# Moving weight loads, bias rows and the output weights' squares along the schedule of a two-layer attention and retention trunk

## Chip, cores and metric

The kernel runs on one core of one Trainium2 chip. The metric is the device time of one execution, in microseconds (us); lower is better. A profile of one execution stands beside the timed runs. Engines: PE is TensorE (matmuls), PEld its weight loads, ACT ScalarE, DVE VectorE, POOL GpSimd, SP SyncE, which here issues nearly all DMAs and so is called the DMA queue.

## What is computed

A sequence of 2048 tokens of width 1024 passes through two layers, and each layer is

```
h = rms_norm(x, norm_gain)                         # over the 1024 columns
aq, ak, av, ag, rq, rk, rv, rg = split(h @ w_in)   # eight sections of 512 columns
A = softmax(aq ak^T / 8 + bias, band) av           # 8 heads of 64, chunks of 64, own chunk + 8 before
B = rms_norm(retention(rotary(rq), rotary(rk), rv))# 4 heads of 128, decaying state, per head
x = x + concat(A * silu(ag), B * silu(rg)) @ w_out
```

and a last RMS norm follows. The bias of a head depends on the distance between two tokens, clipped at 256, and is looked up in a small table. Sums are wanted at float32 accuracy.

## The kernel before

**Numbers in two halves.** Matmuls run in float16. Every float32 operand is scaled by a power of two and split into an upper half and a rest (whT and wlT, hTh and hTl), and three products replace one: upper by upper, upper by rest, rest by upper. So each weight section needs, before its use, a load of 512 KB into a staging ring of three buffers (w4, L46), a square with its sum (sumsq, L308: ACT writes the squares at L312), a sum over partitions on PE and a scale (allsum, L322), and a conversion: upper half on ACT (L333), rest on DVE (L336).

**Stages.** The projection is cut into four slices s of the sections (each two attention heads and one retention head) and four strips n of 512 tokens. For each layer l, slice s and strip n there are two stages: dense_T(l,s,n) (L624; queries and keys, transposed; matmuls at L748) and dense_V(l,s,n) (L755; values and gates; L767). Each has four groups of 24 matmuls 128x512, yields after a third of a group, and so has 12 rounds. After the last slice comes the output projection wout (L1071, matmuls at L1110), which reads the finished rows y (tiles yyy, of 128 tokens), squares, scales, splits and transposes them, and multiplies with the output weights whO and wlO.

**Rounds.** run (L1157) goes through the rounds of a stage. In each it runs what is due of the deferred pieces (later, L607; tick, L610), one step of the attention and retention of the stage before (attention, L793; retention, L879), and then pulls steps from generators that were handed over with push (L1133), evenly over the number of rounds given as run's last argument. The engines PE, ACT, DVE and POOL execute in the order in which the program was written by these rounds; each is in order. SP is ordered by a scheduler, which may draw a DMA ahead to where its buffer is free, unless the DMA was marked to stay in program order (in_turn, L593). SP itself is also in order: a DMA that waits for its source or its buffer holds up all behind it, and each also waits until its lane, one of eight, is free.

**One attention unit** (three rounds) makes 128x640 scores S on PE into a single PSUM buffer (L815, L816), adds the bias on DVE (L819), takes the exponential on ACT (L822), copies to float16 (L824, ACT), takes the rest (L825, POOL), transposes both halves by DMA into pT (L827, SP), and multiplies with the values two units later (L835 to L837). The bias tile of a head is built by a DMA that lays the table out in DRAM (toep, L567), a DMA that reads it with a skewed pattern, two memsets and a scaling on ACT (bias_tiles, L574). **One retention tile** (six rounds) makes a product on PE, masks it (L888), splits it into dT (ACT L873, DVE L877) and uses it a few rounds on as an operand at L869; the state's halves sh go through the same lines.

**Who is pushed where** (main loop, L1377 and on). At n = 1, prep_T (L385) of the next slice, or prep_O(0) (L521) after the last: the four weight sections of dense_T, or the first half of the output weights. At n = 3, prep_V (L417) of the next slice, or prep_O(1). At s = 2, n = 2, prep_Omax (L497): it reads the first 1024 columns of w_out in eight loads of 512 KB, squares each, adds the sums on DVE (L507, L509), and makes the scale of the output weights. At s = 3, n = 3, wout_first (L1058): it loads the first two rows tiles of y, squares, scales and splits them and transposes the first (y_turn, L971). tables (L83) makes the rotary sines and cosines in slice 0.

Of the kernel before, what the change touches and what calls it, by code (L numbers as in the profile page):

```python
# [27 lines left out]
def hybrid_trunk(ctx: ExitStack, tc: tile.TileContext, x, pos, gain, gcol, w_in, w_out, rel, fgain,  # L28
# [54 lines left out]
    def tables(n, wk):  # L83

        ang, k, r, k2 = wk
        pi = k2.bitcast(I32)
        for hf in range(2):
            o = n * 512 + hf * 256
            sp.dma_start(pi[hf * 64:(hf + 1) * 64, :], pos[None, o:o + 256].to_broadcast([64, 256]))
        yield  # L90

        def mulsub(dst, kk, c):
            dve.scalar_tensor_tensor(out=dst, in0=kk, scalar=-c, in1=dst, op0=ALU.mult, op1=ALU.add)

        def rnd(dst, src, mul):
            dve.tensor_scalar(dst, src, mul, MAGIC, op0=ALU.mult, op1=ALU.add)
            dve.tensor_scalar(dst, dst, -MAGIC, None, op0=ALU.add)

        act.activation(ang, pi, AF.Copy, scale=invf_sb[:, 0:1])
        yield  # L100
        rnd(k, ang, 1.0 / P1)
        yield
        for c in (PA, PB, PC):
            mulsub(ang, k, c)
            yield
        dve.scalar_tensor_tensor(out=k2, in0=k, scalar=-(PD + PE_), in1=ang, op0=ALU.mult, op1=ALU.add)
        yield
        rnd(k2, k2, 1.0 / TWO_PI)
        yield
        for kk, c in ((k2, QA), (k, PD), (k2, QB), (k, PE_), (k2, QC)):  # L110
            mulsub(ang, kk, c)
            yield
        dve.tensor_scalar(ang, ang, PI_CL, -PI_CL, op0=ALU.min, op1=ALU.max)
        yield
        dve.scalar_tensor_tensor(out=k, in0=ang, scalar=-1.0, in1=ang, op0=ALU.mult, op1=ALU.max)
        yield
        act.activation(r, ang, AF.Sin)
        act.activation(k2, k, AF.Sin, scale=-1.0, bias=quarter[:, 0:1])
        yield
        act.activation(ang, r, AF.Copy, scale=-1.0)  # L120
        yield
        for hf in range(2):
            sl = slice(hf * 64, hf * 64 + 64)
            cs = slice(hf * 256, hf * 256 + 256)
            sp.dma_start(tab_d[n][0, 0:64, cs], k2[sl, :])
            sp.dma_start(tab_d[n][0, 64:128, cs], k2[sl, :])
            sp.dma_start(tab_d[n][1, 0:64, cs], ang[sl, :])
            sp.dma_start(tab_d[n][1, 64:128, cs], r[sl, :])
        tab_done.add(n)
        yield  # L130
# [158 lines left out]
    TSEC = (0, 1, 4, 5)  # L289
    VSEC = (2, 6, 3, 7)  # L290

    def load_sec(src, nm, halves=False):

        v = src.rearrange("(k p) c -> p k c", p=P)
        if not halves:
            st = w4.tile([P, KT, P], F32, tag="w4", name=f"st{nm}")
            sp.dma_start(st, v)
            return [(st, 0, KT)]
        h = KT // 2
        st = [b2.tile([P, 3 - i, 512], F16, tag=("rot2", "rot3")[i], name=f"st{nm}_{i}") for i in range(2)]  # L300
        st = [t_[:, 0:2].rearrange("p a c -> p (a c)").bitcast(F32).rearrange("p (k c) -> p k c", c=P) for t_ in st]
        for i in range(2):
            sp.dma_start(st[i], v[:, i * h:(i + 1) * h, :])
        return [(st[i], i * h, (i + 1) * h) for i in range(2)]
# [49 lines left out]
    class Sections:  # L354
# [11 lines left out]

        def load(self, j):
            o = TSEC[j] * 512 + self.s * P
            self.sts.append(load_sec(w_in[self.l, :, o:o + P], f"{self.nm}{j}", self.halves))

        def square(self, j):
            nm = f"{self.nm}{j}"
# [12 lines left out]
    def prep_T(l, s, g, halves=False, w=None):  # L385
        w = w or Sections(l, s, g, halves)
        w.load(0)
        yield
        for j in range(4):
            if j < 3:  # L390
                w.load(j + 1)
            yield
            w.square(j)
            yield
            yield
            yield
            w.scale(j)
            yield from w.split(j)
# [122 lines left out]
    def prep_O(l, c, g, go):  # L521
        nm = f"O{l}_{c}"
        g.vh = b3.tile([P, KT, 512], F16, tag="wh", name=f"wh{nm}")
        g.vl = b3.tile([P, KT, 512], F16, tag="wl", name=f"wl{nm}")
        sts = [load_sec(w_out[l, :, c * 512:c * 512 + P], f"{nm}0")]
        yield
        for j in range(4):
            if j < 3:
                o = c * 512 + (j + 1) * P
                sts.append(load_sec(w_out[l, :, o:o + P], f"{nm}{j + 1}"))  # L530
            yield from convert(sts[j], g.vh[:, :, j * P:(j + 1) * P], g.vl[:, :, j * P:(j + 1) * P], go.os)
# [75 lines left out]
    def later(k, fn):  # L607
        deferred.append([k, fn])
# [449 lines left out]
    def wout_first(l, go, us):  # L1058
        us.append(y_load(l, 0))
        x_load(l, us[0])  # L1060
        us.append(y_load(l, 1))
        u, v = us
        for fns in ((), (lambda: y_squares(l, u),), (lambda: y_scale(u, go),), (lambda: rows_hi(u.rows, u.y, u.sy),),
                    (lambda: rows_lo(u.rows, u.y, u.sy), lambda: y_squares(l, v)), (lambda: y_turn(u), lambda: y_scale(v, go)),
                    (lambda: rows_hi(v.rows, v.y, v.sy),), (lambda: rows_lo(v.rows, v.y, v.sy),)):
            yield
            for fn in fns:
                fn()
        yield

    def wout(l, go, gc, us, wT=None):  # L1071

# [303 lines left out]
    for l in range(DEPTH):  # L1376
        gO = [Grp(), Grp()]  # L1377
        go = Grp()
        for s in range(NSW):
            g = grp(l, s)  # L1380
            for n in range(NS):
                first = (l, s, n) == (0, 0, 0)
                if not first:
                    st = St()
                    states[l, s, n] = st
                    dT = dense_T(l, s, n, g, st)
                else:
                    st = st0
                if n == 0 and not first:
                    bs, bt = bias_scratch(l, s), bias_tiles(l, s, g)  # L1390
                    later(1, lambda bs=bs: next(bs))
                    for k in (6, 10, 17, 21):
                        later(k, lambda bt=bt: next(bt))
                if (l, s) == (0, 0) and 0 < n < NS - 1:
                    if n == 1:
                        push(t1, TAB_STEPS - 7)
                    pairs = [xs0[0], w4.tile([P, D], F32, tag="w4", name="rows8") if n == 1 else xs0[1]]
                    pairs = [(w_[:, 0:D], w_[:, D:2 * D]) for w_ in (r_.bitcast(F16) for r_ in pairs)]
                    push(norms_from_input(range(4 * n + 4, 4 * n + 8), late[0:4] if n == 1 else None, pairs,
                                          tables(n + 1, [xs0[n + 1][:, i * 256:(i + 1) * 256] for i in range(4)])), 21)  # L1400
                if (l, s, n) == (0, 1, 1):
                    for l_ in range(1, DEPTH):
                        gr = gain_scale(l_)
                        later(2, lambda gr=gr: next(gr))
                        later(10, lambda gr=gr: next(gr))
                        later(18, lambda gr=gr: next(gr))
                if n == (NS - 1 if (l, s) == (0, 0) else 1):
                    if s + 1 < NSW:
                        push(prep_T(l, s + 1, grp(l, s + 1)), 25)
                    else:  # L1410
                        push(prep_O(l, 0, gO[0], go), 9)
                if n == NS - 1 and s == 1 and l + 1 < DEPTH:
                    gain_load(l + 1)
                if not first:
                    run(dT, att, 10 if n == 0 else 14 if (l, s, n) == (0, 0, NS - 1) else 22 if (l, s) == (0, 0) else 24)
                if n == NS - 1 and s == NSW - 1:
                    us = []
                    push(wout_first(l, go, us), 10)
                if n == 2 and s == 2:
                    push(prep_Omax(l, go), 13)  # L1420
                if n == NS - 1:
                    if s + 1 < NSW:
                        push(prep_V(l, s + 1, grp(l, s + 1)), 23)
                    else:
                        push(prep_O(l, 1, gO[1], go), 9)
                run(dense_V(l, s, n, g, st), att, 24 if n == NS - 1 and s < NSW - 1 else 12)
                if first:
                    sp_order.__exit__(None, None, None)
                    ring["free"] = True
                if att[0] is not None:  # L1430
                    drain(att[0])
                att = [attention(l, s, n, g, st, states.get((l, s, n - 1)))]
# [84 lines left out]
```

## Time and profile before

| | us |
|---|---|
| median of 3 runs | 2080.15 |
| lowest and highest | 2079.01, 2080.17 |
| profiled execution, own time | 2082.83 |
| its span | 2081.1 |
| PE busy | 2006.5 (96% of the span) |
| DVE, ACT, POOL busy | 1229.8, 1139.5, 683.5 |
| mean granted TensorE clock | 0.991 |
| PE waits for pT from DMA | 12.3, in 11 waits |

Times inside the profile count from the span's start. The stages that matter here start at: dense_V(0,1,0) 280.5, dense_T(0,2,2) 563.4, dense_V(0,2,2) 589.3, dense_T(0,3,3) 823.0, dense_V(0,3,3) 849.0, the output projection of layer 0 877.9, dense_T(1,1,0) 1268.8, dense_T(1,2,0) 1474.8, dense_V(1,2,2) 1604.8. A group's row gives line, engine, operation, written and read tiles, and the number and length of its instructions; in a timeline the last bracket is the time for which the engine had been idle and what it waited for. SPq in a timeline is the issue of a DMA on SP, not its transfer; "DMA to landing" is the time from issue to the end of the transfer.

### The profile page before, as it was taken

The numbers are of one execution on the slowest core, as the hardware profiler recorded it, in microseconds if no ns is written. First come the engines' busy times: TensorE is split into PE (matmuls) and PEld (weight loads), VectorE is DVE, ScalarE is ACT, GpSimd is POOL, SyncE is SP. The second block draws the span as 40 slices with busy tenths as digits, with TensorE's granted clock in tenths as the row PEclk, the third lists the DMA queues.
The fourth block names the chain that finished last, engine by engine and source line by source line (L and its number), as shares of the span: only waits on it lengthen the run. The fifth ranks groups of instructions, "written<-read, shape, count | busy, mean of one in ns | idle before, by whom it ended". The sixth has DMA issues, their size and how long they took to land.

```text
span 2081.1 us, 39317 instructions
## 1 busy us (share of the span) xinstructions
PE 2006.5 (96%) x14014; PEld 1052.0 (51%) x14014; DVE 1229.8 (59%) x3817; ACT 1139.5 (55%) x2530; POOL 683.5 (33%) x701
## 2 busy tenths in 40 slices
PE   6988999999999999998999999999999999999998
PEld 4444545555555555544444555555555555554543
DVE  7776556566556555576653556555655565557643
ACT  7566665556565644555443546554655565446432
POOL 0244343444334434430002333444334334343100
PEclk9999999999999999999999999999999999999999
DMA  8678674547484854799765546554755776548874
GB/s 237 162 153 180 142 148 112 114 110 164 117 182 113 167 137 102 153 234 260 203 163 118 125 104 148 120 126 103 152 111 128 178 146 161 127 102 192 211 199 125
DMA packets 645701, 313.63 MB, mean 151 GB/s; under 512 B 459232, under 2 KB 602080, under 8 KB 645504
## 3 DMA queue, kind: packets, MB, share of 16 engines
q1 hardware_dynamic: 645504, 311.12, 65.5%
q8 instruction: 109, 1.79, 0.4%
q14 instruction: 88, 0.72, 0.1%
HBM read 123.26 MB, written 41.98 MB: 79 GB/s over the span
## 4 chain that ended last, share of the span: by engine, by line
PE 49%; DMA 2%; ACT 2%; DVE 1%; issue 0%; SPq 0%; POOL 0%; POOLq 0%; ACTq 0%; DVEq 0%
PE dT L748 15%; PE dV L767 14%; PE dO L1110 13%; PE r L869 2%; DMA pT<-pq 1%; PE S L816 1%; PE S L815 1%; PE o L835 1%; PE o L836 1%; PE o L837 1%; ACT stO1m L312 0%; ACT sc L822 0%; PE ptn L1011 0%; DVE sc L819 0%; ACT pq L824 0%
## 5 line engine op out<-in xcount | busy, mean ns | idle before, releaser
L825 POOL TENSOR_TENSOR pq<-sc,pq 128x640 f16<-128x640 f32 (+4 forms) x256 | 319.6, 1248 | 872.1 <-ACT pq L824 460.2
L822 ACT ACTIVATE sc<-sc,mq,cT 128x640 f32<-128x640 f32 (+4 forms) x256 | 218.4, 853 | 629.4 <-DVE rl L841 338.3
L767 PE MATMUL dV<-whV,hTh 128*128 128x512 f16 x1024 | 353.1, 381 | 4.3 <-DVE gt L785 4.2
L767 PE MATMUL dV<-wlV,hTh 128*128 128x512 f16 x1024 | 353.2, 381 | 0.0
L767 PE MATMUL dV<-whV,hTl 128*128 128x512 f16 x1024 | 353.1, 380 | 0.0
L748 PE MATMUL dT<-hTh,whT 128*128 128x512 f16 x1008 | 349.2, 382 | 2.1 <-DMA hTh<-xa 1.1
L748 PE MATMUL dT<-hTh,wlT 128*128 128x512 f16 x1008 | 348.0, 380 | 0.0
L748 PE MATMUL dT<-hTl,whT 128*128 128x512 f16 x1008 | 347.8, 380 | 0.0
L767 PEld LDWEIGHTS <-hTh 128*128 128x128 f16 x2048 | 196.8, 98 | 219.2 <-DVE gt L785 6.5
L748 PEld LDWEIGHTS <-whT 128*128 128x128 f16 x2016 | 193.0, 98 | 214.9 <-issue 10.6
L819 DVE CUSTOM_DVE_ANT_0 sc<-S,bias 128x640 f32<-128x640 f32 (+4 forms) x256 | 188.3, 736 | 112.7 <-PE S L816 111.3
L1110 PE MATMUL dO<-whO,yly 128*128 128x512 f16 x512 | 194.6, 380 | 1.5 <-DMA yly<-hTl 0.8
L1110 PE MATMUL dO<-whO,yhy 128*128 128x512 f16 x512 | 194.8, 381 | 1.0 <-DMA yhy<-hTh 1.0
L1110 PE MATMUL dO<-wlO,yhy 128*128 128x512 f16 x512 | 194.8, 380 | 0.0
L824 ACT ACTIVATE pq<-sc 128x640 f16<-128x640 f32 (+4 forms) x256 | 171.5, 670 | 8.1
L1110 PEld LDWEIGHTS <-yhy 128*128 128x128 f16 x1024 | 99.9, 98 | 116.1 <-DMA yhy<-hTh 1.5
L767 PEld LDWEIGHTS <-hTl 128*128 128x128 f16 x1024 | 99.3, 98 | 110.6 <-issue 1.9
L748 PEld LDWEIGHTS <-wlT 128*128 128x128 f16 x1008 | 97.5, 98 | 113.1 <-issue 6.2
L815 PE MATMUL S<-k,q 128*128 128x128 f16 (+3 forms) x592 | 142.9, 268 | 0.2
L835 PE MATMUL o<-v,pT 128*128 128x65 f16 x1120 | 130.0, 194 | 12.3 <-DMA pT<-pq 12.3
L836 PE MATMUL o<-v,pT 128*128 128x64 f16 x1120 | 130.2, 195 | 0.0
L816 PE MATMUL S<-k,q 128*128 128x128 f16 (+3 forms) x592 | 130.2, 268 | 0.0
(352 smaller groups left out, 3462.1 us busy)
## 6 DMA issues: line engine op xcount, KB each, us to landing
q<-qq SPq DMA_DIRECT2D x128, 128.0 KB, 2.4
yyy<-y_d SPq DMA_DIRECT2D x32, 512.0 KB, 4.7
stT<-in_w_in_dram SPq DMA_DIRECT2D x27, 512.0 KB, 5.1
stV<-in_w_in_dram SPq DMA_DIRECT2D x26, 512.0 KB, 4.7
k<-kk SPq DMA_DIRECT2D x128, 64.0 KB, 2.0
swp<-rot SPq DMA_DIRECT2D x64, 128.0 KB, 2.7
tabc<-tab SPq DMA_DIRECT2D x32, 256.0 KB, 3.0
tabs<-tab SPq DMA_DIRECT2D x32, 256.0 KB, 3.2
```

What stands on the lines that cost most here:

```text
L748: pe.matmul(ps, w_[:, j, kt, :], h_[:, kt, :], start=(m == 0), stop=(m == 23))
L767: pe.matmul(ps, h_[:, kt, a * P:(a + 1) * P], w_[:, kt, :], start=(m == 0), stop=(m == 23))
L815: pe.matmul(o, st.q[:, hx, 0, cs], k_, start=True, stop=False)
L816: pe.matmul(o, st.q[:, hx, 1, cs], k_, start=False, stop=True)
L819: dve.tensor_tensor_reduce(out=v, in0=S[:, 0:w], in1=g.bias[hx][:, 640 - w:640], scale=1.0, scalar=-3.0e38, op0=ALU.add, op1=ALU.max, accu ...
L822: act.activation(v, v, AF.Exp, bias=m[:, 0:1], scale=g.c[:, 0:1])
L824: act.activation(pq[:, 0:w], v, AF.Copy)
L825: pool.tensor_tensor(pq[:, w:2 * w], v, pq[:, 0:w], op=ALU.subtract)
L835: pe.matmul(o[:, 0:65], u.p[:, b, :], v_[:, 0:65], start=(b == 0), stop=False)
L836: pe.matmul(o[:, 0:64], u.p[:, b, :], v_[:, 65:129], start=False, stop=False)
L869: pe.matmul(out_, w_, m_, start=(i == 0), stop=(i + 1 == len(pairs)))
L1110: pe.matmul(ps, h_[:, kt, :], w_[:, kt, :], start=(m == 0), stop=(m == 23))
```

## The change

Five things move; no instruction is added or taken away on PE, ACT, DVE, POOL or SP.

- **Bias.** With n = 0, the layout of the bias table in DRAM is written two rounds later (3 instead of 1), and the two bias tiles are loaded and scaled one round later in two of four steps (7 and 11 instead of 6 and 10).
- **Held loads.** The first weight load of prep_T and of prep_O(0) is marked to stay in program order, so that the scheduler doesn't draw it ahead into the stage with n = 0; one and two more yields keep the later steps about where they were.
- **Squares of the output weights.** prep_Omax is pushed ahead of dense_T(l,2,2) instead of ahead of dense_V(l,2,2). Its 13 steps then come one a round. The queue's order follows: three of its loads stay where they were, the fourth to eighth go between the transposes, copies and table loads of dense_T, the eighth behind the transpose of the score unit of the fourth.
- **First finished rows.** wout_first is pushed ahead of dense_T(l,3,3) instead of ahead of dense_V; the transpose of the first rows tile is taken out of it and put beside prep_O(1) at round 7 of dense_V(l,3,3).
- **Tables of n = 3.** One yield less in tables: the clamp and the absolute value come in one round, and all behind it a round sooner.

```diff
@@ -111,7 +111,8 @@
             mulsub(ang, kk, c)
             yield
         dve.tensor_scalar(ang, ang, PI_CL, -PI_CL, op0=ALU.min, op1=ALU.max)
-        yield
+        if n < 3:
+            yield
         dve.scalar_tensor_tensor(out=k, in0=ang, scalar=-1.0, in1=ang, op0=ALU.mult, op1=ALU.max)
         yield
         act.activation(r, ang, AF.Sin)
@@ -289,12 +290,14 @@
     TSEC = (0, 1, 4, 5)
     VSEC = (2, 6, 3, 7)
 
-    def load_sec(src, nm, halves=False):
+    def load_sec(src, nm, halves=False, held=False):
 
         v = src.rearrange("(k p) c -> p k c", p=P)
         if not halves:
             st = w4.tile([P, KT, P], F32, tag="w4", name=f"st{nm}")
-            sp.dma_start(st, v)
+            i = sp.dma_start(st, v)
+            if held:
+                in_turn(i)
             return [(st, 0, KT)]
         h = KT // 2
         st = [b2.tile([P, 3 - i, 512], F16, tag=("rot2", "rot3")[i], name=f"st{nm}_{i}") for i in range(2)]
@@ -366,7 +369,8 @@
 
         def load(self, j):
             o = TSEC[j] * 512 + self.s * P
-            self.sts.append(load_sec(w_in[self.l, :, o:o + P], f"{self.nm}{j}", self.halves))
+            self.sts.append(load_sec(w_in[self.l, :, o:o + P], f"{self.nm}{j}", self.halves,
+                                     j == 0 and not self.halves and (self.l, self.s) > (0, 1)))
 
         def square(self, j):
             nm = f"{self.nm}{j}"
@@ -390,6 +394,8 @@
             if j < 3:
                 w.load(j + 1)
             yield
+            if j == 0 and not halves and (l, s) > (0, 1):
+                yield
             w.square(j)
             yield
             yield
@@ -522,8 +528,11 @@
         nm = f"O{l}_{c}"
         g.vh = b3.tile([P, KT, 512], F16, tag="wh", name=f"wh{nm}")
         g.vl = b3.tile([P, KT, 512], F16, tag="wl", name=f"wl{nm}")
-        sts = [load_sec(w_out[l, :, c * 512:c * 512 + P], f"{nm}0")]
-        yield
+        sts = [load_sec(w_out[l, :, c * 512:c * 512 + P], f"{nm}0", held=c == 0)]
+        yield
+        if c == 0:
+            yield
+            yield
         for j in range(4):
             if j < 3:
                 o = c * 512 + (j + 1) * P
@@ -1061,12 +1070,20 @@
         us.append(y_load(l, 1))
         u, v = us
         for fns in ((), (lambda: y_squares(l, u),), (lambda: y_scale(u, go),), (lambda: rows_hi(u.rows, u.y, u.sy),),
-                    (lambda: rows_lo(u.rows, u.y, u.sy), lambda: y_squares(l, v)), (lambda: y_turn(u), lambda: y_scale(v, go)),
+                    (lambda: rows_lo(u.rows, u.y, u.sy), lambda: y_squares(l, v)), (lambda: y_scale(v, go),),
                     (lambda: rows_hi(v.rows, v.y, v.sy),), (lambda: rows_lo(v.rows, v.y, v.sy),)):
             yield
             for fn in fns:
                 fn()
         yield
+
+    def with_turn(gen, us):
+
+        for r in range(12):
+            if r == 7:
+                y_turn(us[0])
+            next(gen, None)
+            yield
 
     def wout(l, go, gc, us, wT=None):
 
@@ -1388,8 +1405,8 @@
                     st = st0
                 if n == 0 and not first:
                     bs, bt = bias_scratch(l, s), bias_tiles(l, s, g)
-                    later(1, lambda bs=bs: next(bs))
-                    for k in (6, 10, 17, 21):
+                    later(3, lambda bs=bs: next(bs))
+                    for k in (7, 11, 17, 21):
                         later(k, lambda bt=bt: next(bt))
                 if (l, s) == (0, 0) and 0 < n < NS - 1:
                     if n == 1:
@@ -1406,23 +1423,24 @@
                         later(18, lambda gr=gr: next(gr))
                 if n == (NS - 1 if (l, s) == (0, 0) else 1):
                     if s + 1 < NSW:
-                        push(prep_T(l, s + 1, grp(l, s + 1)), 25)
+                        push(prep_T(l, s + 1, grp(l, s + 1)), 26 if s else 25)
                     else:
-                        push(prep_O(l, 0, gO[0], go), 9)
+                        push(prep_O(l, 0, gO[0], go), 11)
                 if n == NS - 1 and s == 1 and l + 1 < DEPTH:
                     gain_load(l + 1)
-                if not first:
-                    run(dT, att, 10 if n == 0 else 14 if (l, s, n) == (0, 0, NS - 1) else 22 if (l, s) == (0, 0) else 24)
-                if n == NS - 1 and s == NSW - 1:
-                    us = []
-                    push(wout_first(l, go, us), 10)
                 if n == 2 and s == 2:
                     push(prep_Omax(l, go), 13)
+                last = n == NS - 1 and s == NSW - 1
+                if last:
+                    us = []
+                    push(wout_first(l, go, us), 9)
+                if not first:
+                    run(dT, att, 12 if last else 10 if n == 0 else 14 if (l, s, n) == (0, 0, NS - 1) else 22 if (l, s) == (0, 0) else 24)
                 if n == NS - 1:
                     if s + 1 < NSW:
                         push(prep_V(l, s + 1, grp(l, s + 1)), 23)
                     else:
-                        push(prep_O(l, 1, gO[1], go), 9)
+                        push(with_turn(prep_O(l, 1, gO[1], go), us), 12)
                 run(dense_V(l, s, n, g, st), att, 24 if n == NS - 1 and s < NSW - 1 else 12)
                 if first:
                     sp_order.__exit__(None, None, None)
```

## The prediction

> **What bounds the kernel now.** The page first, its busy times:
>
> ```profile
> PE 2006.5 (96%) x14014; PEld 1052.0 (51%) x14014; DVE 1229.8 (59%) x3817; ACT 1139.5 (55%) x2530; POOL 683.5 (33%) x701
> ```
>
> TensorE is busy for 2006.5 us of a span of 2081.1. The change adds no matmul and takes none away, so what can change is the 74.6 us between matmuls and the pace of the matmuls themselves. Next, therefore, the waits of PE: who waits for what, us in total, times, longest.
>
> ```profile
> PE o L835 <- DMA pT<-pq: 12.3, 11, 2.1
> PE r L869 <- DVE dT L877: 8.1, 9, 2.1
> PE r L869 <- DVE sh L877: 8.1, 5, 4.2
> ...
> PE r L869 <- ACT dT L873: 4.3, 3, 1.5
> PE dV L767 <- DVE gt L785: 4.2, 2, 3.3
> ```
>
> What the change can win is in these: attention probabilities (pT) that come late out of their DMA transpose, and small evacuations on DVE and ACT that are late because something stands ahead of them on their engine. The stretches show where:
>
> ```profile
> 563.40:589.30 25.90, 25.90 (x197) 13.84 (x195) 15.24 (x50) 14.20 (x32) 7.21 (x7) 1.00 0.63 131
> 589.30:618.20 28.90, 26.50 (x208) 14.24 (x206) 15.57 (x51) 20.06 (x47) 13.45 (x13) 1.00 0.85 200
> 823.00:849.00 26.00, 26.00 (x203) 13.95 (x200) 13.59 (x41) 11.25 (x25) 6.57 (x7) 1.00 0.69 132
> 849.00:877.90 28.90, 26.61 (x208) 14.43 (x206) 18.73 (x56) 18.89 (x40) 15.36 (x13) 1.00 0.61 139
> 1604.80:1633.90 29.10, 26.70 (x209) 14.53 (x207) 15.06 (x51) 19.93 (x47) 13.57 (x13) 0.99 0.77 191
> 877.90:930.00 52.10, 48.40 (x358) 25.57 (x356) 36.30 (x103) 28.10 (x52) 14.42 (x12) 0.97 1.04 232
> ```
>
> After the window stand its length, busy PE, PEld, DVE, ACT and POOL, the granted clock, the DMA share and GB/s. Rows 1 and 3, dense_T(0,2,2) and dense_T(0,3,3), are full: PE never rests. The dense_V behind each of them (rows 2 and 4) loses 2.4 and 2.3 us. The change moves work from rows 2 and 4 into rows 1 and 3. By its sum ACT has room there (14.2 and 11.3 of 26); whether it has room by its order decides.
>
> **A. Bias and held weight loads: a gain.** dense_T(1,2,0), SP, then PE; after them the same wait in dense_V(0,1,0), and PE's waits between 1260 and 1310:
>
> ```profile
> 1479.76 1.16 SPq L567 DMA_DIRECT2D toep<-rel_d  x2
> 1481.02 0.53 SPq L297 DMA_DIRECT2D stT<-in_w_in_dram  x1
> 1482.27 4.46 SPq L827 DMA_TRANSPOSE pT<-pq  x1
> ```
> ```profile
> 1491.72 0.20 PE L835 MATMUL o<-v,pT 128*128 128x65 f16 x1 [1.88 <-DMA pT<-pq]
> ...
> 1493.16 0.63 PE L748 MATMUL dT<-hTh,whT 128*128 128x512 f16 x1
> ...
> 1496.56 0.38 PE L748 MATMUL dT<-hTl,whT 128*128 128x512 f16 x1
> 1496.77 0.38 PE L748 MATMUL dT<-hTh,whT 128*128 128x512 f16 x1
> ```
> ```profile
> 290.78 0.20 PE L835 MATMUL o<-v,pT 128*128 128x65 f16 x1 [2.03 <-DMA pT<-pq]
> ```
> ```profile
> PE o L835 <- DMA pT<-pq: 1.4, 1, 1.4
> ```
>
> Two bias copies and a weight load stand on SP ahead of the transpose; its issue takes 4.46 us, and PE stops for 1.88. The eight matmuls from 1493.16 to 1496.56 then take 3.40 us, where eight of 0.21 (1496.56 to 1496.77) take 1.7: another 1.7 lost. dense_V(0,1,0) loses 2.03 and, I assume, the same 1.7; dense_T(1,1,0) loses 1.4. Together 1.88 + 1.7 + 2.03 + 1.7 + 1.4 = 8.7 us. The change puts the copies behind this transpose and the weight load at the end of dense_V. The bias loads and their scaling follow a round later; their first reader is the first score unit of the next attention, more than twenty rounds on, so that costs nothing unless SP falls a whole stage behind. What is late next is a transpose that now has two weight loads right ahead of it, the last of the attention beside n = 0:
>
> ```profile
> 516.17 4.59 SPq L827 DMA_TRANSPOSE pT<-pq  x2
> ```
> ```profile
> 522.79 0.19 PE L835 MATMUL o<-v,pT 128*128 128x65 f16 x1
> ```
>
> PE reads that pT at 522.79. Issued at about 516.2 plus 1.0 for the loads (0.53 each), with the 4.46 of the first fence and landing at once, it is there at 521.7 and costs nothing; at a median landing of a weight load, 5 us behind its issue, it comes at up to 524, 1.2 late. In six places that is 0 to 7; I take 0.5 each, 3.0, nearer to the transposes' own row. A gives **−5.7** (−8.7 to −1.7).
>
> The Trainium skill, "TensorE: Matmul & The Clock Gate", section "What's actually happening", has the clock fall to half after an idle window of about 3.4 us and return after as long a busy one. The 3.40 us of slow matmuls agree with its second half; the stop of 1.88 us ahead of them is shorter than its first half asks for.
>
> **B. The output weights' squares a stage sooner: a loss.** Eight loads of 512 KB, eight squares on ACT and eight adds on DVE go from dense_V(l,2,2) to dense_T(l,2,2). Removed is what the old place loses: 28.90 − 26.50 = 2.4 us in layer 0; in layer 1 the same (29.10 − 26.70), and about 1.7 for a slow stretch behind (clock 0.99): **−6.5**. What is added is order. The squares as they run now, and the engines in the stage that gets them (ACT, DVE, POOL, SP, PE):
>
> ```profile
> L312 ACT ACTIVATE stO0m<-stO0m x8: 1039/1042/1058, 595.0 to 614.2; 128x1024 f32<-128x1024 f32 x8
> L312 ACT ACTIVATION_READ_ACCUMULATOR stO0m<-stO0m x8: 185/187/190, 596.0 to 615.1; 128x1 f32 x8
> ...
> DMA to landing us min/median/max: 4.1/4.8/7.3
> ```
> ```profile
> 572.55 0.18 ACT L930 ACTIVATION_READ_ACCUMULATOR r<-r 128x1 f32 x1
> 572.64 0.57 ACT L647 ACTIVATE qq<-dT 128x512 f16<-128x512 f32 x1
> 573.12 0.26 ACT L873 ACTIVATE dT<-r 128x128 f16<-128x128 f32 x1
> 575.99 0.92 ACT L822 ACTIVATE sc<-sc,mq,cT 128x640 f32<-128x640 f32 x1 [2.61 <-DVE rl L841]
> 576.94 0.74 ACT L824 ACTIVATE pq<-sc 128x640 f16<-128x640 f32 x1
> 577.58 0.29 ACT L917 ACTIVATE state<-state 128x128 f32<-128x128 f32 x1
> 577.78 0.58 ACT L664 ACTIVATE kk<-dT 128x512 f16<-128x512 f32 x1
> ```
> ```profile
> 574.62 0.28 DVE L877 SCALAR_TENSOR_TENSOR dT<-dT,r 128x128 f16<-128x128 f16 x1
> 574.82 0.82 DVE L819 CUSTOM_DVE_ANT_0 sc<-S,bias 128x640 f32<-128x640 f32 x1
> ```
> ```profile
> 577.80 1.40 POOL L825 TENSOR_TENSOR pq<-sc,pq 128x640 f16<-128x640 f32 x1 [3.49 <-ACT pq L824]
> ```
> ```profile
> 573.38 1.32 SPq L827 DMA_TRANSPOSE pT<-pq  x1
> ```
> ```profile
> 588.80 0.28 PE L869 MATMUL r<-rv,dT 128*128 128x128 f16 x2
> ```
>
> A square is 1.04 + 0.19 = 1.23 us. Its staging ring has three buffers, ACT, DVE and SP run in order, and in the changed order the pieces hang on each other. The first square follows the read at 572.73 and ends at 573.96; the two evacuations behind it (0.57, 0.26) and the second square bring ACT to 576.0. On DVE the second add stands ahead of the evacuation dT and of the score (0.28 + 0.82: 577.1); exponential and copy (0.92 + 0.74: 578.8), third square (580.0), state (0.29) and fourth square (581.5), kk (0.58), fifth square (583.3). The fifth add stands ahead of the next score (0.82: 584.1); then 1.66 on ACT (585.8), 1.40 on POOL (587.2), and the transpose of that score on SP (1.32: 588.5). **The eighth load stands behind this transpose**: issued by 589.0 (0.53), it lands 4.8 us later, at 593.8; its square ends at 595.0, and on DVE the eighth add stands ahead of the last evacuation dT (0.28: 595.3). PE's retention product, at 588.80 in its queue, needs that. PE has nothing to go on with, since everything behind it is in order: it stops for 595.3 − 588.8 = 6.5 us, and for about 2 more because DVE has small instructions between these that I left out (three passages of 0.6 to 0.7): **8.5 us** in each layer. From below: the eight squares took 20.3 us from 595.0 to 615.3 in the old place; begun at 572.7 they end at 593.0, a stop of 4.5. From above: all at the longest landing, 7.3, 2.5 more: 11. I take 8.5, since the chain is counted link by link. Behind so long a stop I add the slow stretch of 1.7. Two layers: 2 × 10.2 = 20.4 (12.4 to 25.4), and with the 6.5 removed B gives **+13.9** (+5.9 to +18.9). The weight loads of prep_V behind the eight come sooner on SP and cost nothing as long as they follow the eighth. If the loads didn't gate, the squares' 9.8 us would fit in ACT's 11.7 free ones of row 1.
>
> **C. First output rows in dense_T(l,3,3).** Row 4 loses 2.3 us a layer to evacuations behind other ACT work. Row 3 has 14.7 free us of ACT, and the two loads stand where they did, long ahead, so no square hangs on a load as in B. But the conversions of prep_O(1) fill the place that comes free. Half of 2 × 2.3: **−2.3** (−4.6 to 0; more late transposes of y would make it a loss of at most the 2.1 of the longest pT wait).
>
> **D. Rotary tables of n = 3.** The table loads of ACT leave the place ahead of gt, where PE waits 3.3 us; their stores move on SP ahead of a pT, up to 2.1 by that group. From −3.3 to +2.1, I take **−0.5**.
>
> **E. Start of the output projection.** Two y loads and one transpose go out sooner. The pT waits that A leaves are 12.3 − 5.3 = 7.0 us, some of them here; but the DMA engines are full there (share 1.04), so sooner for one is later for another: **−1.0** (−5 to +2).
>
> **Sum.** −5.7 + 13.9 − 2.3 − 0.5 − 1.0 = +4.4 us. The profiled execution took 2082.83 us (span 2081.1 and 1.7 around it), 2.7 above the median of the runs, 2080.15; so 2087.2 against its own time, and for the median 2080.15 + 4.4, rounded **2084.6**. A measurement of this kernel can tell about 0.2% from no change, 4.2 us, so the forecast lies just at that edge, on the slow side.
>
> **Rivals.**
> 1. *The loads keep pace.* If the eighth load lands before about 587.5, which needs the fourth to eighth out some 6 us sooner than counted, the stop in dense_T(l,2,2) is gone. For it: row 1 has a DMA share of 0.63 and ACT has room. Against: the order on SP is fixed, and each link has its row. B is then −6.5, the sum −16.0: 2064. Between the two (stops of 3 us, no slow stretch: B −0.5) it is −10: 2070. Faster.
> 2. *The gains come whole.* B as counted, but the new transposes cost nothing, C is at its end, and D and E win 2 each: 13.9 − 8.7 − 4.6 − 2 − 2 = −3.4: 2076.8. The few pT waits of other stages, all under 2.1, speak for it.
> 3. *Saturation.* Eight loads, the tables' and prep_V's in one stage take the landing to 7.3; row 6 shows a full DMA system at 232 GB/s, and five more loads in row 1 (2.6 MB in 26 us, 101 GB/s) bring its 131 to 232. B +18.9, sum +9.4: 2089.6; with late transposes in all six places (+4) 2094.
> 4. *The slow stretches aren't due to the short stops.* Then they stay: A −2.3, B +15.6, sum +9.5: 2089.7. The rows, where each stop of about 2 us has them behind it, speak against it. That would be the rule of the skill's page.
> 5. *It doesn't do what it says*: the scheduler's order on SP leaves the transposes behind the copies. The changed order shows them moved; 2080 to 2090.
>
> **How the numbers follow.** Forecast 0.48; rival 1 0.16; rival 2 0.16; rival 3 0.12; rival 4 0.05; rival 5 0.03. The forecast with its own uncertainty lies within 0.2% (2076.0 to 2084.3) in some 4 of 10 of its cases, above in the rest; rival 2 is mostly within, at times faster. Faster by over 0.2%: 0.16 + 0.06 = 0.22. Within: 0.48 × 0.4 + 0.10 = 0.29. Slower: 0.49. The range, 2066 to 2094, takes in the upper half of rival 1 and all of rivals 2 to 4; the forecast's own is 2077 to 2092.
>
> **What would show it.** Right: in dense_T(0,2,2) of the changed profile, or at its very end, a wait of PE r on DVE dT of 6 to 11 us with L312 stO0m squares ahead of it and their loads landing after 590; no waits on pT in the two n = 0 stages of layer 1; dense_V(0,2,2) near 26 us. Wrong: that stretch full, as row 1 is now; or the pT waits merely moved to the end of dense_V with n = 0. C is right if dense_V(0,3,3) loses under 1.5 us.

## The result, and the profile after

| | before | changed |
|---|---|---|
| median of 4 runs, us | 2079.58 | 2096.52 |
| lowest, highest | 2078.61, 2080.17 | 2093.69, 2101.23 |
| profiled execution, own time | 2082.83 | 2101.23 |
| its span | 2081.1 | 2099.4 |

The changed kernel is slower: ratio 1.0080, 95% interval 1.0058 to 1.0102, about 16.6 us. The profiled execution is the slowest of the four, so the stages below add up to 18.3 us and not to 16.6. The prediction had the direction, but 2084.6 was too low by 12 us, and the measured time lies 2.5 us outside its range.

First the busy times of the changed kernel, for comparison with the first fence of the prediction, then PE's longest waits in it:

```profile
PE 2008.5 (96%) x14014; PEld 1052.9 (50%) x14014; DVE 1225.5 (58%) x3817; ACT 1139.0 (54%) x2530; POOL 686.3 (33%) x701
```
```profile
PE o L844 <- DMA pT<-pq: 20.3, 17, 5.0
PE r L878 <- ACT dT L882: 14.5, 4, 6.5
PE r L878 <- DVE dT L886: 11.6, 9, 2.8
PE r L878 <- DVE sh L886: 6.1, 4, 4.1
```

PE is busy for 2.0 us more, though it does the same matmuls; some of them ran slower. The waits on pT, which the bias' move was to shorten, went from 12.3 us in 11 to 20.3 in 17. The wait on the evacuation dT on ACT (L882, L873 before) went from 4.3 to 14.5. The stretches of the changed kernel say where (length, busy PE, PEld, DVE, ACT, POOL, granted clock, DMA share, GB/s):

```profile
282.40:308.30 25.90, 25.90 (x204) 14.21 (x202) 16.30 (x54) 16.13 (x37) 14.82 (x17) 1.00 0.54 104
308.30:334.00 25.70, 24.06 (x167) 12.17 (x165) 13.07 (x66) 11.93 (x31) 4.02 (x6) 1.00 0.81 177
565.00:602.30 37.30, 27.15 (x198) 14.08 (x196) 13.71 (x54) 20.81 (x44) 6.45 (x6) 0.93 0.86 193
602.30:630.90 28.60, 28.60 (x208) 15.46 (x206) 16.03 (x59) 15.74 (x39) 14.96 (x14) 0.91 0.41 98
862.00:889.20 27.20, 26.33 (x209) 14.48 (x207) 18.94 (x46) 16.01 (x35) 15.73 (x13) 1.00 0.82 167
1484.80:1510.90 26.10, 26.10 (x205) 14.01 (x203) 16.41 (x56) 16.64 (x42) 6.68 (x6) 1.00 0.79 172
1585.50:1623.60 38.10, 27.32 (x198) 14.07 (x196) 13.72 (x54) 20.82 (x44) 6.46 (x6) 0.92 0.88 187
```

Two rows of the kernel before that the prediction doesn't show, dense_V(0,1,0) and dense_T(1,2,0), to be held against rows 1 and 6:

```profile
280.50:310.30 29.80, 27.77 (x205) 14.70 (x202) 17.26 (x54) 16.97 (x40) 15.03 (x16) 0.94 0.70 122
1474.90:1504.80 29.90, 28.02 (x206) 14.44 (x204) 18.10 (x61) 18.75 (x45) 7.00 (x8) 0.94 0.82 174
```

- Rows 3 and 7, dense_T(l,2,2), hold the loss: 37.3 us in place of 25.9, and 38.1 in place of 25.9.
- Row 4, dense_V(0,2,2), is as long as before (28.6 against 28.9), but for another reason. PE is busy for all of the 28.60 us and the clock is 0.91: nothing waits, but its first matmuls are slow. The granted clock is 0.50 from 597.3 to 607.4, that is from within the stop in row 3 until 5.1 us into row 4, and 1.00 from 607.5 on.
- Rows 1 and 6, dense_V(0,1,0) and dense_T(1,2,0), show A's gain: 25.9 in place of 29.8, 26.1 in place of 29.9. Row 2, dense_T(0,1,1), shows a part given back: it was 23.7 us long.
- Row 5, dense_V(0,3,3), is C's gain: 27.2 in place of 28.9. The dense_T(0,3,3) ahead of it, which got the work, stays at 26.0.

By stages, each from its first large matmul to that of the next, the two profiles differ by: squares +21.2 (dense_T(l,2,2) +11.4 and +12.2, the two stages behind each −2.4 in all); bias and loads −2.3 (−9.8 in stages with n = 0, +7.4 in the stages behind); first output rows −3.2; the stages up to dense_V(0,0,3) +1.9; the second output projection +1.3; dense_V(1,0,0) −0.5. Together that is 18.4; the spans differ by 18.3.

**The chain in dense_T(0,2,2).** ACT's waits for loads from 565 to 605, and then SP, ACT and PE there:

```profile
ACT stO0m L315 <- DMA stO0m<-in_w_out_dram: 8.7, 4, 3.0
```
```profile
588.90 0.43 SPq L298 DMA_DIRECT2D stO0m<-in_w_out_dram  x1
591.36 3.69 SPq L836 DMA_TRANSPOSE pT<-pq  x1
595.40 0.40 SPq L298 DMA_DIRECT2D stO0m<-in_w_out_dram  x1
```
```profile
596.54 1.06 ACT L315 ACTIVATE stO0m<-stO0m 128x1024 f32<-128x1024 f32 x1 [3.01 <-DMA stO0m<-in_w_out_dram]
...
597.60 0.58 ACT L690 ACTIVATE rot<-dT 128x512 f32<-128x512 f32 x1
598.07 0.27 ACT L882 ACTIVATE dT<-r 128x128 f16<-128x128 f32 x1
599.87 1.06 ACT L315 ACTIVATE stO0m<-stO0m 128x1024 f32<-128x1024 f32 x1 [1.54 <-DMA stO0m<-in_w_out_dram]
```
```profile
598.39 0.40 PE L878 MATMUL r<-rv,dT 128*128 128x128 f16 x2 [6.41 <-ACT dT L882]
...
601.94 0.29 PE L878 MATMUL r<-rv,dT 128*128 128x128 f16 x1 [2.83 <-DVE dT L886]
...
602.34 3.62 PE L776 MATMUL dV<-whV,hTh 128*128 128x512 f16 x8
...
607.76 1.89 PE L776 MATMUL dV<-whV,hTl 128*128 128x512 f16 x8
```

It is the prediction's kind of chain: the eighth load (595.40) stands on SP behind the transpose (591.36), ACT waits for loads, and PE stands at the retention product. But it has more links. ACT waits 8.7 us in all, for the fifth to the eighth load (2.0, 2.1, 3.0 and 1.5). And PE stands twice, for 6.41 and 2.83 us. The longer stop ends with the evacuation dT on ACT (598.07), which stood behind the seventh square (596.54). The load of that square was issued at 588.90, ahead of the transpose, and landed only some 7.6 us later; the DMA share was 1.03 from 589.0 to 591.4 and 1.63 from 591.4 to 595.0. Only the shorter stop hangs on the eighth load. Behind it eight matmuls take 3.62 us (602.34); at full pace they take 1.89 (607.76).

### The profile page after: what moved, and what is told of

The parts are those of the page before. It is cut to its first block, busy times and chain, and to the rows that moved or that the text cites. A ratio compares the mean times of both kernels' runs of the same rounds, so it can differ in the third digit from the quotient of the medians.

```text
span 2099.4 us, 39284 instructions
## 1 busy us (share of the span) xinstructions
PE 2008.5 (96%) x14014; PEld 1052.9 (50%) x14014; DVE 1225.5 (58%) x3817; ACT 1139.0 (54%) x2530; POOL 686.3 (33%) x701
## 5 line engine op out<-in xcount | busy, mean ns | idle before, releaser
L844 PE MATMUL o<-v,pT 128*128 128x65 f16 x1120 | 130.7, 194 | 20.4 <-DMA pT<-pq 20.3
L824 PE MATMUL S<-k,q 128*128 128x128 f16 (+3 forms) x592 | 143.3, 268 | 1.1 <-DVE mq L828 1.1
L844 PEld LDWEIGHTS <-pT 128*128 128x128 f16 x1120 | 106.0, 97 | 58.6 <-DMA pT<-pq 30.4
```

The lines of the kernel that those rows point to most:

```text
L824: pe.matmul(o, st.q[:, hx, 0, cs], k_, start=True, stop=False)
L844: pe.matmul(o[:, 0:65], u.p[:, b, :], v_[:, 0:65], start=(b == 0), stop=False)
```

## The experiments

The theory after the result: the loss is the order of loads, squares and transposes in dense_T(l,2,2), worth about 21 us, and all else together gains a little. Rivals: the squares' own time on ACT, whatever their loads; or the other moves on the DMA queue. Each ratio is to the kernel before in runs on the same chip. The intervals are 0.10% to 0.16% to either side, 2 to 3 us, and 0.22% for the changed kernel; so differences under about 3.5 us between two kernels, and under about 5 us to the changed kernel, are not resolved by the times.

| kernel | what differs | median, us | ratio (95%) |
|---|---|---|---|
| changed | | 2096.52 | 1.0080 (1.0058 to 1.0102) |
| e1 | changed, squares back | 2078.10 | 0.9982 (0.9971 to 0.9993) |
| e2 | before, squares alone | 2102.52 | 1.0092 (1.0076 to 1.0108) |
| e3 | changed, three loads for eight squares | 2073.94 | 0.9956 (0.9941 to 0.9972) |
| e4 | changed, a square in two rounds | 2080.01 | 0.9985 (0.9973 to 0.9997) |
| e5 | e1, weight loads not held | 2072.28 | 0.9956 (0.9944 to 0.9969) |
| e6 | e1, bias as before | 2072.87 | 0.9963 (0.9950 to 0.9977) |
| e8 | changed, loads three ahead | 2083.23 | 1.0013 (1.0003 to 1.0023) |
| e10 | e8 and e5 | 2081.28 | 1.0000 (0.9989 to 1.0011) |
| e11 | before, first rows and tables alone | 2079.36 | 0.9986 (0.9976 to 0.9996) |
| e12 | e5, a square in two rounds | 2072.97 | 0.9962 (0.9948 to 0.9975) |
| e13 | e5, tables as before | 2074.71 | 0.9967 (0.9956 to 0.9977) |

**e1, the squares back.**

```diff
-                if n == 2 and s == 2:
-                    push(prep_Omax(l, go), 13)
                 if not first:
                     run(dT, att, ...)
+                if n == 2 and s == 2:
+                    push(prep_Omax(l, go), 13)
```

> The changed kernel with the squares of the output weights back ahead of dense_V(l,2,2); all else as changed. Theory (the order of loads, squares and transposes in dense_T(l,2,2) is the loss; by the two profiles +21.2 us of +18.6): 2074 to 2078 us, dense_T(0,2,2) full again at 25.9 us, dense_V(0,2,2) 28.9. Rival (the held loads and the earlier tables are half of the loss, by new late transposes): 2083 to 2088.

2078.1 us, at the upper end of what was expected and 20 below the changed kernel (1.0080 − 0.9982), and dense_T(0,2,2) is 25.9 us long again.

**e2, the squares alone**: the reverse edit in the kernel before.

> The kernel before with this part alone: the squares pushed ahead of dense_T(l,2,2). Theory: 2098 to 2102 us, stops of 6 and 3 us on ACT dT and DVE dT at the end of dense_T in both layers. Rival (the stop arises only together with the other moves on the DMA queue): under 2090.

2102.5 us, half a microsecond above the expected range; ratio +0.0092, 19 us. PE's waits from 560 to 632:

```profile
PE r L869 <- ACT dT L873: 6.4, 1, 6.4
PE r L869 <- DVE dT L877: 2.5, 1, 2.5
PE o L835 <- DMA pT<-pq: 0.8, 1, 0.8
PE dT L748 <- DVE kk L667: 0.6, 1, 0.6
PE S L815 <- DVE mq L819: 0.4, 1, 0.4
```

The stop needs none of the other moves. From both sides the squares are worth 19 to 20 us, so the queue rival falls.

**e3, three loads for eight squares.** It leaves out five of the eight loads, so the sum of squares is another.

```diff
-        st = load_sec(w_out[l, :, 0:P], f"{nm}m0")
+        sts = [load_sec(w_out[l, :, j * P:(j + 1) * P], f"{nm}m{j}") for j in range(3)]
         for j in range(KT):
             yield
-            m1 = sumsq(st, f"{nm}m{j}", None)
-            if j + 1 < KT:
-                st = load_sec(w_out[l, :, (j + 1) * P:(j + 2) * P], f"{nm}m{j + 1}")
+            m1 = sumsq(sts[j % 3], f"{nm}m{j}", sts[j % 3][0][0])
```

> The changed kernel, but only the first three of the eight loads are made, and the eight squares read these three tiles in turn (so the sum is that of other numbers: part of the computation is left out). ACT's and DVE's instructions and order stay. Theory (the loads gate): the two stops of 9.2 us together fall to 1 to 4 us, the slow matmuls behind shrink, 2078 to 2084 us. Rival (eight squares of 1.23 us in that stage are too much for ACT in order, whatever their loads): the stop stays over 7 us, 2093 to 2097.

2073.9 us, lower than expected. All eight squares still run in dense_T(0,2,2), in the same place in ACT's order, and of the stop this is left (PE's waits from 560 to 632):

```profile
PE r L876 <- DVE dT L884: 1.5, 1, 1.5
PE o L842 <- DMA pT<-pq: 1.1, 1, 1.1
```

9.2 us have become 1.5: waiting for loads makes five sixths of the stop, ACT's own time the rest. The rival on ACT's time falls. Without five loads the DMA engines also have less to do, so this run alone doesn't tell a late issue from a slow transfer; e8 does.

**e4, a square in two rounds.**

```diff
                 dve.tensor_tensor(mm, mm, m1, op=ALU.add)
+            yield
...
-                    push(prep_Omax(l, go), 13)
+                    push(prep_Omax(l, go), 21)
```

> The changed kernel with one more step behind each square, so that the eight go over dense_T and dense_V of (l,2,2), one in two rounds. Theory: each load has two rounds (4.3 us) and the look-ahead of the ring, the stop in dense_T falls under 2 us and the waits of dense_V (2.4 us) go too: 2072 to 2077 us. Rival (ACT's order, not the loads): stops of 3 to 6 us remain in each layer, 2081 to 2088.

2080.0 us, 3 above the expected range. dense_T(l,2,2) is full (25.9), as the theory has it, but dense_V(l,2,2) takes 30.7 and 31.1 us instead of 28.9 and 29.1. PE's waits from 560 to 632:

```profile
PE o L845 <- DMA pT<-pq: 1.4, 1, 1.4
PE r L879 <- DVE dT L887: 1.3, 2, 0.7
PE o L845 <- DVE rl L851: 0.5, 1, 0.5
PE r L879 <- ACT dT L883: 0.4, 1, 0.4
```

Three late loads and those of prep_V now stand on SP between the transposes of dense_V, and later squares between its evacuations: the wait was spread, not removed.

**e8, loads three ahead.** Same squares and adds, each load asked for as soon as its buffer can be free.

```diff
-        st = load_sec(w_out[l, :, 0:P], f"{nm}m0")
+        sts = [load_sec(w_out[l, :, j * P:(j + 1) * P], f"{nm}m{j}") for j in range(3)]
...
-            m1 = sumsq(st, f"{nm}m{j}", None)
-            if j + 1 < KT:
-                st = load_sec(w_out[l, :, (j + 1) * P:(j + 2) * P], f"{nm}m{j + 1}")
+            m1 = sumsq(sts[j], f"{nm}m{j}", None)
+            if j + 3 < KT:
+                sts.append(load_sec(w_out[l, :, (j + 3) * P:(j + 4) * P], f"{nm}m{j + 3}"))
```

> The changed kernel with the output weights' loads asked for three ahead instead of one ahead; squares, adds and their order as changed, nothing left out. The fifth, sixth and seventh load then stand on the DMA queue ahead of the copies of q and k, and the eighth ahead of the transpose it stood behind. Theory (loads gate through the queue's order): the stops fall from 9.2 us to 2 to 5 in each layer: 2080 to 2088 us. Rival (full DMA engines, not the order, make the loads late): they stay over 7: 2092 to 2098.

2083.2 us, 14 below the changed kernel, as the theory expected. The order on SP is the lever: the same bytes in the same stage, and ACT waits 3.3 us for loads in place of 8.7. But the loads that go out sooner now stand ahead of transposes, and the two dense_T(l,2,2) are still 31.6 and 32.6 us long (PE, 560 to 632):

```profile
PE r L878 <- DVE dT L886: 3.0, 1, 3.0
PE o L844 <- DMA pT<-pq: 2.2, 1, 2.2
```

**e5, loads not held.**

```diff
-                                     j == 0 and not self.halves and (self.l, self.s) > (0, 1)))
+                                     False))
...
-        sts = [load_sec(w_out[l, :, c * 512:c * 512 + P], f"{nm}0", held=c == 0)]
+        sts = [load_sec(w_out[l, :, c * 512:c * 512 + P], f"{nm}0")]
...
-            if j == 0 and not halves and (l, s) > (0, 1):
-                yield
...
-        if c == 0:
-            yield
-            yield
```

(and the 26 and 11 steps of prep_T and prep_O back to 25 and 9)

> e1_squares_back with the weight loads not held (nor the extra yields that go with them); the bias copies and tiles stay later. Theory (in A the gain comes from the copies behind the transpose, and the held loads give 6 to 7 us back as late transposes in dense_T(l,s,1), each 0.4 to 2 us): 2071 to 2075 us, no waits on pT in dense_T(l,s,1). Rival (one load of 512 KB ahead of the transpose is enough to make it late): the stops of about 2 us in the stages with n = 0 come back, 2077 to 2082.

2072.3 us, as expected: no kernel of the table is faster, and it is below both kernels of the change (0.9956, 9 us under the kernel before). Between 278 and 565, where the changed kernel waits for late transposes in dense_T(0,1,1) and dense_T(0,2,1), PE waits for nothing.

**e6, loads held, bias as before** (later(1) and steps 6 and 10).

> e1_squares_back with the bias copies and tiles where they were before; the held loads stay. Theory (both copies ahead of the transpose are what makes it late): stops of 1 to 3 us on pT in stages with n = 0 of layer 1 and slow matmuls behind, and the late transposes of dense_T(l,s,1) as well: 2080 to 2085 us. Rival (the weight load, not the copies): 2076 to 2079, as e1.

2072.9 us. That neither the theory nor its rival expected: the held loads alone do as well as the bias alone. dense_T(1,2,0), SP's issues in e5 (the weight load at the start, the copies behind the transpose) and in e6 (the copies at the start, no load):

```profile
1471.05 0.38 SPq L298 DMA_DIRECT2D stT<-in_w_in_dram  x1
1473.18 1.40 SPq L831 DMA_TRANSPOSE pT<-pq  x1
1474.62 1.23 SPq L571 DMA_DIRECT2D toep<-rel_d  x2
```
```profile
1475.47 1.16 SPq L576 DMA_DIRECT2D toep<-rel_d  x2
1477.99 1.78 SPq L836 DMA_TRANSPOSE pT<-pq  x1
```

The transpose issues in 1.40 us behind the load and in 1.78 behind the two copies. Behind all three, in the kernel before, it took 4.46, and in the four other places of that kernel with the same order 4.15 to 4.97. So the old stop needs both, and to move either is enough. To move both buys nothing more, and the held loads then stand ahead of other transposes. SP in the changed kernel, at the start of dense_T(0,2,1):

```profile
515.63 0.43 SPq L298 DMA_DIRECT2D stT<-in_w_in_dram  x1
516.16 0.54 SPq L859 DMA_DIRECT2D y_d<-ya  x1
516.74 0.43 SPq L298 DMA_DIRECT2D stT<-in_w_in_dram  x1
517.28 5.57 SPq L836 DMA_TRANSPOSE pT<-pq  x2
```

PE waits 1.5 us for the first of these two. In e6, where held loads stand there too, PE's waits on pT from 278 to 565 come to 1.9 us against 2.1 in e1; by the times e1 and e6 differ by 4 us, at the edge of what the times resolve. Why e6 has less of the held loads' price than e1 stays open.

**e10, e8 and e5 together.**

> e8_ahead and e5_bias_only together. Theory: the sum of both effects, 2075 to 2084 us, beneath the kernel before if the stop in dense_T(l,2,2) falls to 2 us or less. Rival: as e8.

2081.3 us, within the expected range and no gain: with the look-ahead, the squares in dense_T(l,2,2) still cost 9 us over e5.

**e11, first rows and tables alone.**

> The kernel before with only the first output rows a stage sooner and the tables' one step (parts C, D and E of the prediction); bias, weight loads and squares as before. Theory (C gives 3 us, D and E nothing that can be told): 2075 to 2078 us, and what it differs from e5_bias_only by, 5 to 8 us, is the worth of the bias' move. Rival (most of the gain of e5_bias_only is in C, D, E): 2071 to 2074.

2079.4 us, 1.4 above the expected range; ratio 0.9986, 2.9 us of gain for C, D and E together; the rival falls. Against it e5 stands 6 us lower, the worth of the bias' move, and e1, with bias and held loads, 0.8 lower, which the times don't resolve.

e11 and e2 leave the bias and the weight loads as they were, and so show how much the old stops vary. In dense_T(1,2,0) the transpose issues in 4.29 us in e11 and in 4.46 in e2, as in the kernel before; but PE stops there for 0.32 and 1.02 us in place of 1.88. dense_V(0,1,0), dense_T(1,1,0) and dense_T(1,2,0) together are 2.5 us longer in e11 than in e5, 4.0 in e2, and 9.2 in the profile of the kernel before.

**e12, e5 with a square in two rounds**, begun with dense_V(l,2,2) and spread over 24 rounds (the edit of e4 and run's last argument).

> e5_bias_only with one square in two rounds, begun with dense_V(l,2,2) as before and running into dense_T(l,2,3). Theory (in the old place too the waits come from squares that stand close ahead of evacuations): dense_V(l,2,2) loses under 1 us in place of 2.8, 2066 to 2070 us. Rival (the later squares put their loads between the transposes of dense_T(l,2,3), as in the changed kernel): 2072 to 2080, with waits on pT there.

2073.0 us, no better than e5, and the rival is right. dense_V(0,2,2) is full (26.1 us), but in dense_T(0,2,3) a weight load of prep_V comes to stand ahead of a transpose, and PE stops for it in dense_V(0,2,3); SP, then PE:

```profile
635.09 0.43 SPq L298 DMA_DIRECT2D stV<-in_w_in_dram  x1
635.63 4.06 SPq L832 DMA_TRANSPOSE pT<-pq  x1
```
```profile
642.34 0.20 PE L840 MATMUL o<-v,pT 128*128 128x65 f16 x1 [2.69 <-DMA pT<-pq]
```

**e13, e5 with the tables as before.**

> e5_bias_only with the tables as before. Theory (D is nothing): 2071 to 2074 us, as e5_bias_only; the wait on gt in dense_V(0,0,2) is back at about 3 us and the one on pT there, 3 to 5 us in the other kernels, is gone. Rival (the tables' step costs by its stores ahead of that transpose): 2067 to 2070.

2074.7 us, 0.7 above the expected range, which the times don't tell from e5. In dense_V(0,0,2) the wait on gt (the gates) is back at 3.27 us and none on pT is left; with the tables sooner gt costs under 0.4, but the transpose there is late by 2 to 5 us. In the changed kernel:

```profile
190.31 0.24 PE L844 MATMUL o<-v,pT 128*128 128x65 f16 x1 [4.99 <-DMA pT<-pq]
```

## Why the prediction was wrong

The direction of the forecast was right, and so was the mechanism in the main: loads held up by the order on SP, squares held up by loads, PE held up by evacuations behind the squares. Two terms of the sum were mis-sized, both to the same side: B by 7 us and A by 3.

- **B, "+13.9": measured 19 to 20 by the times, 21.2 by the stages.** The added part, 2 × 10.2 = 20.4, measured 28.3 by the stages; the removed part, −6.5, measured −7.1. Three steps failed.
  - The chain let only the eighth load gate and put the waits for the loads ahead of it at nothing. ACT also waited for the fifth, sixth and seventh, and the seventh square, not the eighth add, ends the longer stop. The two stops came to 9.2 us where 8.5 were forecast, but this agreement is partly luck. The eighth load went out 30.4 us after the start of the stage, not 25.6; and PE came to the product 1.6 us later than forecast and did a part of it between the two stops.
  - The forecast went from this stop to the length of the stage as if nothing else in it waited. But ACT and DVE, late in the middle of the stage, also held up the PSUM buffers of the scores and of kk (the keys) and a pT, 0.9 us in dense_T(0,2,2) and 1.6 in dense_T(1,2,2); and PE was busy for 27.15 us in place of 25.90 there, in part because the clock fell within the stop.
  - "The slow stretch of 1.7" behind the stop was taken from a stop of 1.9 us, with 3.4 us of slow matmuls behind it. Behind 6.4 and 2.8 they last 5.1 us and cost about 2.5 in dense_V(0,2,2) (28.6 against the full 26.1). Per layer the added part is 14 us, not 10.2.
- **A, "−5.7": measured −0.8 by the times (e1 against e11, not resolved), −2.3 by the stages.** In the two profiles the 8.7 us of old stops went, and the slow stretches with them (rows 1 and 6), as forecast; but that profile had these stops longer than e2 and e11 have them; by the times, e5 against e11, they are worth about 6. The step that failed on the other side is "I take 0.5 each, 3.0": the six stages behind, dense_T(l,s,1) and dense_V(1,3,1), pay 7.4, 0.4 to 2.0 each. The bound (0 to 7) nearly held that value, and the choice in it was wrong: it leaned on the case in which the transpose lands at once. In dense_T(0,2,1) the two transposes take 5.57 us to issue behind the loads, 4.59 before, and PE gets the first pT at 524.4, 7.1 us after its issue began; the upper case of the forecast had 524.
- **C, "−2.3"**: −3.2 by the stages, and −2.9 with D and E by e11. Right within what can be told.
- **D, "−0.5"**: nothing that the times tell; one wait for another (e13).
- **E, "−1.0"**: the second output projection is 1.3 us longer, the first unchanged. No run has E alone; not resolved.

Of the signs that the prediction named, the late loads, the long wait on dT and the missing waits on pT in the n = 0 stages of layer 1 came; dense_V(0,2,2) near 26 us did not (28.6).

The rivals: "the loads keep pace" has the right lever, as e3 and e8 show, but not in this order. "The gains come whole" fails at the 7.4 us that the stages behind pay in A, and at B. "Saturation" gives nearly the right loss for B (+18.9), but it is not the main cause: the squares' loads land after 4.6 us at the median, 4.8 before, with a DMA share of 0.86, and e8 shows that most are late because they are issued late. It has a part in the seventh load, which took 7.6 us; landing after the median 4.6 it would have let its square begin 3.0 us sooner. In e8 that load lands after 4.5 us and ACT waits 1.1 for it. "The slow stretches aren't due to the short stops" is refuted by rows 1 and 6, where both the stops of 2.03 and 1.88 us and their slow stretches are gone: here the measurement differs from the idle window of about 3.4 us in the Trainium skill, "TensorE: Matmul & The Clock Gate", section "What's actually happening". But not each stop has such a stretch behind it: after the same stop of 3.26 us on gt in dense_V(0,0,2), the matmuls soon turn slow in the kernel before (0.63 us each in place of 0.38), and in e2 they run at a clock of 1.00.

## What to carry to other kernels

Room on an engine by its sum says little where queues are in order: before work goes into a full stage, follow its loads through the DMA queue to the first instruction behind them that the busy engine needs, ask of each load, and not only of the last, when it lands, and then list everything else that hangs on the late engine. A move that takes DMAs away from one transfer puts them ahead of another; price the new neighbour by a row in which such a pile stands ahead of such a transfer. Where a delay needs two causes, remove the one that has a free place to go. A stop read from one profile is one draw: look for it in other runs that leave its place as it was before it is priced.

## What the runs showed of the hardware

- The issue of one DMA transpose on SP grew sharply with what was issued just ahead: 1.40 us behind one load of 512 KB, 1.78 behind two copies of 384 KB, 4.46 behind both (e5, e6, before), 4.06 behind two table loads and a weight load (e12).
- A stage can be longer with no wait in it: dense_V(0,2,2) of the changed kernel has PE busy for 28.60 of 28.60 us at a clock of 0.91, after the stops of the stage ahead. The price of a stop is then found in the next stage's row, not beside the wait.
- Loads of 512 KB landed after 4.45 to 7.62 us in one stage (the fourth to the eighth in dense_T(0,2,2) of the changed kernel).
